# One gathered latent tile in layer 0, and context's retrieval moved ahead of most of the latents' mixer, in a two-layer hybrid trunk

## The chip, the cores and the metric
One NeuronCore of a Trainium2 chip runs the whole program in one launch. The metric is device time in microseconds of one execution, the median of three runs. Less is better. PE is TensorE, DVE is VectorE, ACT is ScalarE, POOL is GpSimd and SP is SyncE, which issues most of the DMAs.

## The reference, cut to what matters
512 latent tokens and 256 context tokens of width 1024 pass two layers. Each layer is a token mixer followed by a PEER feed-forward; both add to the stream through a gate. In layer 0 the mixer is differential attention beside an HGRN2 recurrence. Context reads context alone; latents read both. In layer 1 only the latents go on.

```python
def block(xb):                       # 128 tokens
    q = (xb @ w_q).reshape(P_TOKEN_BLOCK, P_HEADS, 2, P_DQ // 2)
    s = jnp.einsum('nhpd,hpkd->nhpk', q, keys).astype(jnp.float32)
    s_top, i_top = lax.top_k(s, P_TOPK)
...
    gate = jax.nn.softmax(best, axis=-1)
    u = u_tab[idx]
    v = v_tab[idx]
    act = jax.nn.gelu(jnp.einsum('nd,nhkd->nhk', xb, u).astype(jnp.float32), approximate=False)
    return jnp.einsum('nhk,nhkd->nd', (gate * act).astype(v.dtype), v)
```

Eight heads pick 16 experts each, so a token uses 128 of 16,384 experts. An expert is one row of 1024 floats in `u_tab` and one in `v_tab`.

## The kernel before, in words
Everything is float32. A matmul is made of three, over a rounded high part and a rest of each operand (`split`, L221: ScalarE copies the high part, VectorE or POOL subtracts it). `chunk` (L334) loads a 128-column block of a weight matrix (512 KB) on SP's queue and splits it; with `LOS` "p" the rest comes from POOL.

**Two ways through PEER.** *Dense*: for each of 128 blocks j of 128 experts, `expert_in` (L1841) forms gelu(u.x) for all dense tokens (a "u step": 24 matmuls as wide as the dense tokens), the result is multiplied by a gate matrix G, and `peer_out` (L1850) multiplies it with the block's rows of v (an "output step"). G comes from `spread` (L1663), which builds two one-hot matrices for each token on VectorE and ScalarE and multiplies them on PE. 96 of the 128 u steps of layer 0 are done early ("spilled") and stored in AD. *Gathered*: `sparse` (L1693) handles one tile of 128 tokens. For each of its 128 expert slots it gathers one row per token from u (128 x 1024 floats, 512 KB, an indirect DMA that POOL issues, L1711), and one VectorE instruction forms the dot products (L1723). Then the same for v, with an accumulating instruction (L1733). A tile so takes 256 steps, called rows here. `take` (L1716) keeps NS rows in flight.

`GT` says how many latent tiles of a layer are gathered: (0, 2). Context's two tiles are always gathered. With no gathered tile all 512 tokens are dense, and `peer_out` takes its form `full`: 18 matmuls for the first 768 output columns and, by `roll` (L1869), 6 more for the last 256. Otherwise each dense tile of 128 tokens takes 6 matmuls of 512 columns in an output step.

**What sets the order.** Each mixer, tail and retrieval is a generator that yields between pieces. `merge` (L580) takes the next piece from the one that is least far along for its weight. `pull(n)` (L457) emits n further rows of the gathered tiles, first tile first. The engines run in the order that the compiler gives them; each works its own instructions in order.

In `even` (L470) the latents' mixer has four HGRN2 units of 16 steps (64) and four attention units of 7 (28). Beside it runs `tail` (L536): context's output projection (8 steps), its normalisation (1), its retrieval (`retrieve` L1554: 8 heads, then 16 decoding steps), 33 in all. The weights decide who comes first:

```python
left = s.weave([(tail(), TL), (hg, TW * 64), (da, TW * 28)], True)
...
s.rate = RX
s.weave([(hg, left[1]), (da, DF * left[2])])
```

With TW = 3 the mixer ends after 11 steps of the tail; the remaining 22 follow alone. Gathering of context begins only then. `mix_out` (L610) projects the latents and pulls RX = 2 rows in each of its 8 steps.

In `peer(0)` (L1748) the retrieval of four latent tiles pulls 2 x R0 rows at each of its 8 heads. Its other yields carry a price (3.6 for a head of a tile, 2.6 for one of four decoding steps of a tile, 1.2 for one of 32 spreading steps); each time the price passes UP = 5.5 a u step is emitted with R0 rows. The other early u steps follow with RT rows each. `peer_out` spreads what is left evenly.

## Time and profile before

| | us |
|---|---|
| median of 3 runs | 5414.69 |
| runs | 5413.29 to 5420.99 |
| profiled execution | 5428.23 |
| its span, first to last instruction | 5426.4 |
| PE busy | 4376.8 (81%) |
| DVE busy | 4042.6 (74%) |
| POOL busy | 2880.2 (53%) |
| ACT busy | 1924.7 (35%) |

A matmul's duration in the profile holds its passage through the array, which overlaps the next one's. Busy time counts overlapping instructions once. Idle time is put down to what ended it. Times of stretches are from the span's start.

### The profile page before, as it was taken

The page shows a single profiled execution, that of the slowest core. Times are in us where ns is not written, and L with a number is a line of the kernel's source. Part 1 is how long each engine was busy: PE and PEld are TensorE (multiplying, and loading weights), DVE is VectorE, ACT ScalarE, POOL GpSimd, SP SyncE. Part 2 cuts the span into 40 slices and gives each one's busy share as a digit, 9 for nine tenths or more (in the row PEclk, how much of TensorE's full clock was granted, in tenths as well). Part 3 has the DMA queues.
Part 4 walks back from the last instruction along what each step waited for, and adds up shares of the span by engine and source line. Part 5 has one row for each costly group of instructions (what it writes and reads, how often), then busy time and mean ns, then how long its engine had stood idle before and what let it go on. Part 6 is the DMA issues. An engine that isn't in the chain of part 4 may idle for free. (4 is left out here: it accounts for less than half of the span.)

```text
span 5426.4 us, 72537 instructions
## 1 busy us (share of the span) xinstructions
PE 4376.8 (81%) x25323; PEld 3525.1 (65%) x25323; DVE 4042.6 (74%) x8314; ACT 1924.7 (35%) x3942; POOL 2880.2 (53%) x1967
## 2 busy tenths in 40 slices
PE   7889987787877888888898899897947546777766
PEld 5766666566766767777777677785746546555555
DVE  4555669789998546777777676662799987988887
ACT  3444443234553322222222356342415332222222
POOL 2232223564445675655565311442475668899885
PEclk8889998898988999999999999997968777888888
DMA  5431124566657888887788511004376788999996
GB/s 193 138 99 60 58 68 157 195 201 239 222 203 246 294 287 288 281 279 276 268 286 279 186 42 45 16 6 149 100 255 226 277 298 311 345 347 342 347 357 252
DMA packets 450414, 1155.56 MB, mean 213 GB/s; under 512 B 42112, under 2 KB 185856, under 8 KB 446464
## 3 DMA queue, kind: packets, MB, share of 16 engines
q1 hardware_dynamic: 302304, 612.94, 33.9%
q0 software_dynamic: 147744, 537.99, 27.6%
q8 instruction: 200, 3.28, 0.2%
q14 instruction: 166, 1.36, 0.1%
HBM read 1052.20 MB, written 98.57 MB: 212 GB/s over the span
## 5 line engine op out<-in xcount | busy, mean ns | idle before, releaser
L228 POOL TENSOR_TENSOR wlo<-wraw,whi 128x1024 fp32r<-128x1024 f32 x405 | 1003.9, 2482 | 1150.4 <-ACT whi L225 1073.0
L1733 DVE SCALAR_TENSOR_TENSOR sacc<-ga,sact,sacc 128x1024 f32<-128x1024 f32 x508 | 754.8, 1486 | 333.0 <-DMA ga<-in_pv,idx 327.4
L248 PE MATMUL u<-hh,wlo 128*128 128x512 f32 (+1 forms) x2048 | 755.7, 369 | 194.1 <-POOL wlo L228 193.9
L1723 DVE SCALAR_TENSOR_TENSOR ga<-ga,htok 128x1024 f32<-128x1024 f32 x512 | 741.9, 1462 | 203.2 <-DMA ga<-in_pu,idx 202.5
L245 PE MATMUL u<-hh,whi 128*128 128x512 f32 (+1 forms) x2048 | 758.9, 371 | 156.1 <-ACT act L1847 65.3
L1711 POOL DMA_INDIRECT ga<-in_pu,idx x512 | 673.7, 1316 | 356.4 <-DVE ga L1723 103.4
L225 ACT ACTIVATE whi<-wraw 128x1024 fp32r<-128x1024 f32 x415 | 437.1, 1055 | 1093.0 <-PE u L246 490.2
L1711 POOL DMA_INDIRECT ga<-in_pv,idx x512 | 641.9, 1254 | 299.4 <-DVE sacc L1733 121.1
L246 PE MATMUL u<-hl,whi 128*128 128x512 f32 (+1 forms) x2048 | 747.5, 365 | 0.0
L248 PEld LDWEIGHTS u<-hh,wlo 128*128 128x128 f32 x2048 | 435.0, 213 | 256.7 <-POOL wlo L228 214.6
L245 PEld LDWEIGHTS u<-hh,whi 128*128 128x128 f32 x2048 | 435.3, 213 | 226.8 <-ACT act L1847 75.6
L246 PEld LDWEIGHTS u<-hl,whi 128*128 128x128 f32 x2048 | 434.3, 212 | 40.4
L225 ACT ACTIVATE vh<-vraw 128x768 fp32r<-128x768 f32 (+1 forms) x256 | 243.1, 950 | 606.1 <-PE acc L1953 404.2
L1954 PE MATMUL acc<-wh,vl 128*128 128x512 f32 x768 | 314.9, 410 | 69.5 <-DVE vl L228 69.4
L228 DVE TENSOR_TENSOR vl<-vraw,vh 128x768 fp32r<-128x768 f32 (+1 forms) x256 | 334.7, 1307 | 12.4 <-ACT vh L225 12.4
L1688 PE MATMUL g<-ohB,ohA 128*128 128x128 f32 x1536 | 259.1, 308 | 98.4 <-DVE ohB L1686 75.1
L1952 PE MATMUL acc<-wh,vh 128*128 128x512 f32 x768 | 310.3, 405 | 11.0 <-ACT wh L225 11.0
L1688 PEld LDWEIGHTS g<-ohB,ohA 128*128 128x128 f32 x1536 | 227.8, 213 | 135.8 <-issue 57.2
L1953 PE MATMUL acc<-wl,vh 128*128 128x512 f32 x768 | 310.5, 404 | 3.4 <-POOL wl L228 3.4
L1969 PE MATMUL acc<-vl,wh 128*128 128x512 f32 x512 | 223.0, 463 | 109.5 <-DVE vl L228 109.3
L1686 DVE TENSOR_SCALAR ohB<-c_all,pt 128x128 f32<-128x128 f32 x768 | 273.8, 397 | 14.6 <-PE g L1688 12.6
L228 POOL TENSOR_TENSOR wl<-ad,wh 128x512 fp32r<-128x512 f32 (+1 forms) x176 | 235.7, 1340 | 58.0 <-ACT wh L225 56.0
(506 smaller groups left out, 9774.0 us busy)
## 6 DMA issues: line engine op xcount, KB each, us to landing
wraw<-in_uT SPq DMA_DIRECT2D x256, 512.0 KB
vraw<-in_pv SPq DMA_DIRECT2D x256, 512.0 KB
wraw<-in_ada_w SPq DMA_DIRECT2D x96, 512.0 KB
G<-stg SPq DMA_DIRECT2D x24, 2048.0 KB
wraw<-in_ew SPq DMA_DIRECT2D x64, 512.0 KB
G<-G SPq DMA_DIRECT2D x32, 1024.0 KB
wraw<-in_pwq SPq DMA_DIRECT2D x48, 512.0 KB
AD<-act SPq DMA_DIRECT2D x96, 256.0 KB
```

The lines of the kernel that those rows point to most:

```text
L225: nc.scalar.activation(hi, x, AF.Copy)
L228: i = (lo_eng or nc.vector).tensor_tensor(lo, x, hi.bitcast(F32), OP.subtract)
L245: nc.tensor.matmul(o, a, hh[:, k], start=(k == 0), stop=False)
L246: nc.tensor.matmul(o, a, hl[:, k], start=False, stop=False)
L248: nc.tensor.matmul(o, b, hh[:, k], start=False, stop=(k == nk - 1))
L1688: nc.tensor.matmul(ps[:, n], A, B, start=True, stop=True)
L1711: nc.gpsimd.indirect_dma_start(out=ga, out_offset=None, in_=tab, in_offset=bass.IndirectOffsetOnAxis(ap=idx[:, k:k + 1], axis=0))
L1723: nc.vector.scalar_tensor_tensor(ga, ga, 1.0, htok, op0=OP.mult, op1=OP.mult, accum_out=act[:, k:k + 1])
L1733: nc.vector.scalar_tensor_tensor(acc, ga, act[:, k:k + 1], acc, op0=OP.mult, op1=OP.add)
L1952: nc.tensor.matmul(acc[d], a, wh, start=st, stop=False)
L1953: nc.tensor.matmul(acc[d], a, wl, start=False, stop=False)
L1954: nc.tensor.matmul(acc[d], b, wh, start=False, stop=sp)
```

## The change
Layer 0 gathers one latent tile of four, so 384 tokens are dense and `full` no longer holds. TW falls from 3 to 0.4: the whole tail is woven with the first two fifths of the latents' mixer. `weave` returns the steps taken; the rest of the mixer runs with RX = 3.5 rows pulled after every step, and the projection with RM = 4 rows a step. Rows in flight: NS from (3, 5) to (4, 7); layer 0's PEER adds NP = 3 buffers and its output steps NX = 3 (before 1); `take` now looks as far ahead as there are buffers. In `spread` the small tile pt moves from the pool of six buffers to one of two. R0 and RT of layer 0 rise from 2 to 2.5.

```diff
--- before.py
+++ after.py
@@ -25,16 +25,17 @@
 SPILL = (96, 80)
 JG = 4
 UP = (5.5, 4.0)
-GT = (0, 2)
-R0 = (2.0, 2.5)
+GT = (1, 2)
+R0 = (2.5, 2.5)
 RG = (2, 1)
 NR = 2
 NV = 3
 VQ = 'sync'
 OH = "av"
 VERB = 0
-TW = 3
-RX = 2.0
+TW = 0.4
+RX = 3.5
+RM = 4.0
 NE = 6
 ND_ = 3
 PW = 2
@@ -42,12 +43,12 @@
 DL = 8
 LA = 3
 NA = 3
-NX = 1
+NX = 3
 ROB = 1e-5
 MORE = tuple(tuple(int(c) for c in x) for x in '11,11'.split(','))
 MOREP = tuple(tuple(int(c) for c in x) for x in '00,00'.split(','))
 TP = 3.6
-RT = (2, 2.5)
+RT = (2.5, 2.5)
 LOS = 'ppv,p,p,p,p,p,p'.split(',')
 NG = (1, 1)
 SQ = 'sync'
@@ -61,7 +62,8 @@
 MO = tuple(int(c) for c in '00')
 UB = 2
 AH = 2
-NS = (3, 5)
+NS = (4, 7)
+NP = (3, 0)
 TB = 32
 
 
@@ -546,7 +548,7 @@
                         yield from s.mix_out(mps, s.stream(YC, L), L, yh, yl, I['ewo'], put)
                         yield from s.ctx_peer(cx, mps, psp)
                     with s.more(*M2):
-                        left = s.weave([(tail(), TL), (hg, TW * 64), (da, TW * 28)], True)
+                        took = s.weave([(tail(), TL), (hg, TW * 64), (da, TW * 28)], True)
                 sp1 = s.side.enter_context(tc.tile_pool(name="sp1", bufs=NS[0], side="right"))
                 s.sp2 = s.side.enter_context(tc.tile_pool(name="sp2", bufs=1, side="right"))
                 s.gpools = [sp1] * NS[0]
@@ -557,8 +559,9 @@
                 s.gens = [s.sparse(0, s.sp2, s.pick[i], s.HT[i], keep(i)) for i in range(2)]
                 for g in s.gens:
                     next(g)
-                s.rate = RX
-                s.weave([(hg, left[1]), (da, DF * left[2])])
+                for _ in s.merge([(hg, max(1, 64 - took[1])), (da, max(1, 28 - took[2]))]):
+                    s.pull(RX)
+                s.rate = RM
             if s.until == 'diff':
                 nc.sync.dma_start(out=s.O['y'], in_=YX)
                 return
@@ -600,7 +603,7 @@
         done = [0] * len(gens)
         for _ in s.merge(gens, until, done):
             pass
-        return [max(1, n - b) for (_, n), b in zip(gens, done)]
+        return done
 
     def add_to(s, x, g):
         def put(d, ps):
@@ -1660,13 +1663,13 @@
             yield from decode(i)
             yield from after(i)
 
-    def spread(s, p, sp, psp, gps, pick, tb0, G):
+    def spread(s, p, p2, sp, psp, gps, pick, tb0, G):
 
         nc, C = s.nc, s.C
         tp = s.t(psp, [128, 3, 128], tag='hs')
         for i in range(3):
             s.flip(tp[:, i], pick[i].rearrange("p a b -> p (a b)"))
-        pt = s.t(p, [128, 3, 128], tag='pt')
+        pt = s.t(p2, [128, 3, 128], tag='pt')
         nc.scalar.activation(pt, tp, AF.Copy)
         for b in range(128 // TB):
             stg = s.t(sp, [128, 128, TB], tag='stg')
@@ -1715,7 +1718,7 @@
 
         def take(tab, k):
 
-            while len(ahead) < NS[l] and k + len(ahead) < 128:
+            while len(ahead) < len(s.gpools) and k + len(ahead) < 128:
                 ahead.append(fetch(tab, k + len(ahead)))
             return ahead.pop(0)
         for k in range(128):
@@ -1770,6 +1773,8 @@
                 sp1 = ent(tc.tile_pool(name=s.name("sp1"), bufs=NS[l]))
                 s.sp2 = ent(tc.tile_pool(name=s.name("sp2"), bufs=1))
                 s.gpools, s.turn = [sp1] * NS[l], 0
+            if NP[l]:
+                s.gpools = s.gpools + [ent(tc.tile_pool(name=s.name("spx"), bufs=NP[l]))] * NP[l]
             HT = tc.dram_tile([max(ng, 1), 128, D], F32, name=s.name('HT'))
 
             old = [j for j in range(128) if (j + 1) * spill // 128 > j * spill // 128]
@@ -1810,6 +1815,7 @@
                 def done():
                     et.close()
                     eg.append(ee(tc.tile_pool(name=s.name("pe2"), bufs=NE, side="right")))
+                    eg.append(ee(tc.tile_pool(name=s.name("pe3"), bufs=2, side="right")))
                     eg.append(ee(tc.tile_pool(name=s.name("pe1"), bufs=NG[l], side="right")))
 
                 def after(i):
@@ -1820,7 +1826,7 @@
                                                lambda acc: s.add_tok(psu, 'u', acc, s.xl, t0, gl)))
                         next(s.gens[-1])
                         return
-                    yield from s.spread(eg[0], eg[1], psm, gps, s.pick[i], t0 // TB, G)
+                    yield from s.spread(*eg, psm, gps, s.pick[i], t0 // TB, G)
                 price, n = 0.0, 0
                 for p in s.retrieve(l, ep, tp_, pk, (psq, 'q'), (psm, 'hs'), (hh, hl), tiles, 1 if ctx else ng, done, after):
                     price += p
@@ -1861,7 +1867,7 @@
                 tc.tile_pool(name=s.name("ad"), bufs=ND_) as ad, \
                 tc.tile_pool(name=s.name("ppo"), bufs=1, space=PSUM) as pso:
             acc = [s.t(pso, [128, 512], tag=f'acc{i}') for i in range(6 if full else ND // 64)]
-            s.gpools = s.gpools + [sp3] * NX
+            gpools, s.gpools = s.gpools, s.gpools + [sp3] * NX
             s.rate = s.left() / (128.0 + 128 - len(old)) + 0.02
             dm = 768 if full else D
             prev = []
@@ -1971,7 +1977,7 @@
                             nc.tensor.matmul(acc[2 * t + e], b, vh[:, e * 512:e * 512 + 512], start=False, stop=sp)
                 s.pull(s.rate)
             s.pull(1 << 20)
-            s.gpools = s.gpools[:NS[l]]
+            s.gpools = gpools
             if full:
                 roll(1, pend)
                 for d in range(6):
```

## Rows read from the trace of the kernel before

**Rows 1.** Eight stretches: length, busy us (instructions) by engine, clock, DMA share, GB/s
```profile
340.00:862.00 522.00, 474.42 (x2626) 349.27 (x2624) 322.83 (x820) 227.55 (x459) 146.30 (x77) 0.96 0.22 67
862.00:965.00 103.00, 76.49 (x455) 62.81 (x456) 99.55 (x379) 24.94 (x47) 32.74 (x15) 0.80 0.49 170
965.00:1800.00 835.00, 657.49 (x3176) 529.92 (x3176) 730.75 (x2077) 355.46 (x878) 433.68 (x264) 0.88 0.66 223
1800.00:2035.00 235.00, 208.21 (x886) 164.80 (x885) 106.40 (x100) 63.33 (x94) 175.37 (x103) 0.97 0.88 297
2035.00:3060.00 1025.00, 918.31 (x3803) 740.17 (x3804) 746.68 (x907) 262.29 (x440) 579.64 (x428) 0.95 0.81 278
...
3830.00:4490.00 660.00, 417.57 (x2565) 380.77 (x2563) 614.70 (x1657) 240.19 (x554) 406.85 (x246) 0.80 0.70 238
4490.00:4580.00 90.00, 59.58 (x332) 54.79 (x332) 62.08 (x38) 17.47 (x25) 79.92 (x48) 0.79 0.89 304
4580.00:5390.00 810.00, 596.68 (x2630) 474.62 (x2631) 718.37 (x704) 238.74 (x349) 696.84 (x485) 0.85 0.95 344
```

**Rows 2.** POOL groups, 340 to 862: count | busy us, mean ns | idle before <-releaser
```profile
L228 POOL TENSOR_TENSOR wlo<-wraw,whi 128x1024 fp32r<-128x1024 f32 x50 | 121.9, 2439 | 301.6 <-ACT whi L225 268.8 <-issue 18.7 <-PE hs L799 9.4
```

**Rows 3.** Groups of instructions, 965 to 1800
```profile
L1723 DVE SCALAR_TENSOR_TENSOR ga<-ga,htok 128x1024 f32<-128x1024 f32 x128 | 198.4, 1553 | 54.9 <-DMA ga<-in_pu,idx 54.6
...
L1686 DVE TENSOR_SCALAR ohB<-c_all,pt 128x128 f32<-128x128 f32 x499 | 168.2, 378 | 10.8 <-PE g L1688 9.4 <-ACT pt L1670 0.2
...
L1685 DVE TENSOR_SCALAR ohA<-c_all,pt 128x128 f32<-128x128 f32 x249 | 75.1, 308 | 1.0 <-PE g L1688 0.4
...
L1733 DVE SCALAR_TENSOR_TENSOR sacc<-ga,sact,sacc 128x1024 f32<-128x1024 f32 x43 | 69.1, 1606 | 27.2 <-DMA ga<-in_pv,idx 27.0
...
L1847 ACT ACTIVATE act<-u 128x512 f32<-128x512 f32 x61 | 35.6, 584 | 0.0
```

**Rows 4.** Groups of instructions, 1800 to 2035
```profile
L1733 DVE SCALAR_TENSOR_TENSOR sacc<-ga,sact,sacc 128x1024 f32<-128x1024 f32 x71 | 93.9, 1323 | 128.4 <-DMA ga<-in_pv,idx 127.1
...
L228 POOL TENSOR_TENSOR wlo<-wraw,whi 128x1024 fp32r<-128x1024 f32 x35 | 85.0, 2429 | 11.8 <-ACT whi L225 11.2
...
L1847 ACT ACTIVATE act<-u 128x512 f32<-128x512 f32 x36 | 20.9, 580 | 4.1 <-issue 4.1
```

**Rows 5.** Groups of instructions, 2035 to 3060, VectorE
```profile
L1733 DVE SCALAR_TENSOR_TENSOR sacc<-ga,sact,sacc 128x1024 f32<-128x1024 f32 x140 | 193.6, 1383 | 116.2 <-DMA ga<-in_pv,idx 114.6
...
L1723 DVE SCALAR_TENSOR_TENSOR ga<-ga,htok 128x1024 f32<-128x1024 f32 x128 | 163.3, 1295 | 104.4 <-DMA ga<-in_pu,idx 104.4
...
L228 DVE TENSOR_TENSOR vl<-vraw,vh 128x768 fp32r<-128x768 f32 x126 | 139.1, 1104 | 0.5 <-ACT vh L225 0.5
...
L1878 DVE SCALAR_TENSOR_TENSOR xl<-u,g,xl 128x512 f32<-128x512 f32 x126 | 93.6, 743 | 3.8 <-PE u L1876 3.8
...
L228 DVE TENSOR_TENSOR rl<-vraw,rh 128x256 fp32r<-128x256 f32 x124 | 91.7, 778 | 0.0
```

**Rows 6.** Timeline near 1838: start, us, engine, line, operation
```profile
1838.01 2.52 POOL L228 TENSOR_TENSOR wlo<-wraw,whi 128x1024 fp32r<-128x1024 f32 x1 [1.37 <-ACT whi L225]
...
1838.18 2.63 DVE L228 TENSOR_TENSOR rl<-vraw,rh 128x256 fp32r<-128x256 f32 x1
```

**Rows 7.** Timeline of PE, two matmuls, the second 22 after the first
```profile
2408.93 0.39 PE L245 MATMUL u<-hh,whi 128*128 128x512 f32 x1
...
2413.92 0.39 PE L1953 MATMUL acc<-wl,vh 128*128 128x512 f32 x1
```

**Rows 8.** Instructions on tile rl: duration ns min/median/max, first and last start
```profile
L228 DVE TENSOR_TENSOR rl<-vraw,rh x128: 407/414/2629, 1834.5 to 3050.8; 128x256 fp32r<-128x256 f32 x128
```

**Rows 9.** DMA issues by line, with count and KB of each
```profile
G<-G SPq DMA_DIRECT2D x32, 1024.0 KB
...
ad<-AD SPq DMA_DIRECT2D x96, 256.0 KB
```

**Rows 10.** Windows, one slice of layer 1
```profile
4352.00:4488.00 136.00, 69.87 (x442) 66.55 (x443) 118.38 (x187) 45.72 (x118) 84.27 (x62) 0.71 0.84 297
```

## The prediction

> **What bounds the kernel now.** I read the busy times by stretch first [rows 1]. They follow the program: latents' mixer with context's projection beside it (340 to 862), context's retrieval and the latents' output projection (862 to 965), layer 0's PEER in three parts (965 to 1800 retrieval and one-hot spreading, 1800 to 2035 the rest of the 96 spilled u steps, 2035 to 3060 the 128 output steps), and for comparison three stretches of layer 1, which already gathers two of its four tiles. The reader is to see that each part has another bound. 340 to 862 is PE's (474 of 522 us) while VectorE is at 62% and DMA at 0.22. 862 to 1800 is VectorE's (99.6 of 103, 731 of 835). 2035 to 3060 is PE's (918 of 1025). 4580 to 5390, where PE has less to do, is DMA's: share 0.95 at 344 GB/s.
>
> Next come the groups of instructions [rows 3 to 5]. Every gathered row costs VectorE one pass over 1024 elements, POOL one issue and DMA 512 KB. 128 + 43 rows run before 1800, 71 before 2035, and the remaining 270 after (268 in the two groups, two first ones apart). VectorE waits for landing rows: 55 + 27 us, 127 us of 235, and 104 + 115 us [rows 3 to 5]. The queue is three rows deep there.
>
> **The change, part by part.** Sums are made against the profiled execution, 5428.2 us, which lies 13.5 us above the median of 5414.7.
>
> *Mixer and context (340 to 965, now 625 us).* Latent mixer steps number 64 + 28 = 92; the context tail has 33. With weights 0.4 x 64 and 0.4 x 28 the tail ends beside 26 + 11 = 37 steps, leaving 55, each followed by 3.5 rows: 193 rows.
> First part: PE 474.4 x 37/92 = 191, and at most the 76.5 of 862 to 965 [rows 1], 267 together, at the 0.91 busy share of 340 to 862: 290 us. VectorE has 130 + 99.6 = 230 in it and fits beside. The tail's loads, splits and stores are moved ahead of most of the mixer's on SP and POOL: DMA at 0.22 and POOL at 28% hide them; if that cover were gone, the 24 splits would cost 24 x 2.44 = 59 us [rows 2].
> Second part: PE has only 474.4 x 55/92 = 284. VectorE has 322.8 x 55/92 = 193 and 193 rows x (1.295 + 0.08) = 266; 0.08 is my allowance for reading the accumulator. That is 459, and 495 us at the 0.93 busy share of 3830 to 4490 [rows 1], where rows fill the gaps of other VectorE work. Below it is bounded by full hiding, 470 at a share of 0.977. Above, no hiding: 55 x 522/92 + 266 = 578. I take 495, nearest to the stretch that mixes the two kinds of work.
> Here a row matters: a VectorE split of 256 elements, 0.41 us at the median [rows 8], took 2.63 us when it started 0.17 us behind a POOL split, and ended 0.1 us after it [rows 6]. Two-input work on the two engines takes turns. The duration of 1.295 has such waits in it, from a stretch with POOL at 57%.
> The Trainium skill, GPSIMD Engine Reference, section 1 (Specifications), says that GpSimd shares its SBUF interfaces with VectorE and contends with VectorE instructions of two SBUF inputs, as the rows' are. The trace agrees [rows 6]. Counted in full, that rule would add the 19 weight splits of this part, 19 x 2.44 = 46 us, so 505 instead of 459, 542 instead of 495, and no gain in the sum.
> Output projection: 103 us now, PE 76 busy, its adds waiting behind the retrieval on VectorE. Without the retrieval but with 32 rows (44 us of VectorE): 85.
> 290 + 495 + 85 = 870 against 625: **+245**.
>
> *Retrieval and u steps (965 to 2035, now 1070 us).* One tile fewer is spread: a quarter of 168.2 + 75.1 [rows 3], 61 us of VectorE. By the prices of the yields, 3 x 8 x 3.6 + 4 x 4 x 2.6 + 3 x 32 x 1.2 = 243, 44 u steps fit in at 5.5 each. Rows: 8 x 5 at the projections and 44 x 2.5, so 150 instead of 171: 21 x 1.57 = 33. Together 94, or 107 at the 0.875 share. Lookahead grows from 3 to 7; half of the 82 us of waiting should go, 40. 835 - 147 = 688, call it 690. 52 u steps with 130 rows follow, against 36 steps now [rows 4]. A step now takes 235/36 = 6.5 us. It will hold 2.5 rows. POOL: 175.4/36 = 4.9 now, which with half a row of 1.2 more is 5.5. DMA: 3.5 x 512 + 192 KB = 2.03 MB, at 344 GB/s 5.9. PE: 24 matmuls of 384 columns, 4.1. I take 6.0, 312 us; 5.5 and 6.5 are the ends (286 to 338). 690 + 312 = 1002: **-68**. The new transposes, copies and eight 64 KB stores of the gathered tile fall in the normalisation and are counted below.
>
> *Output steps (2035 to 3060, now 1025 us).* Matmuls of 512 columns follow one another every 4.99/22 = 0.227 us [rows 7]. Now 24 a step and 24 more in 32 of them. Afterwards 18 a step and 24 of 384 columns (0.17 us, scaled): 128 x 18 x 0.227 + 32 x 24 x 0.17 = 654 us against 871. VectorE loses the rolled adds and small splits (93.6 + 91.7) and a third comes onto its large ones (139.1 x 1/3 = 46) [rows 5]: 747 becomes about 600. Rows left: 768 - (193 + 32) - (150 + 130) = 263, so VectorE keeps that load. DMA [rows 9]: 128 x (512 + 192) + 96 x 192 + 32 x 512 + 263 x 512 KB = 266 MB, which at 344 GB/s is 773 us, now the largest. Ten rows ahead should keep it fed. I take 800; 773 is the lower end. **-225**.
>
> *Rest.* Closing copies, transposes and adds of three dense tiles, and the gathered tile's preparation: about **+10**, an estimate. Layer 1: lookahead 5 becomes 7, then 10. VectorE waited little there and DMA is at 0.95 in 4580 to 5390: **-10**, between -45 and +10. Moving pt to a two-buffer pool and larger NX, NP only take memory; pt is written once a tile, so nothing waits.
>
> Sum: 245 - 68 - 225 + 10 - 10 = -48. 5428.2 - 48 = 5380; less 13.5, about **5367 us** in the median's terms.
>
> **The rivals.** *Rows stand in line with the mixer (slower).* A POOL gather waits until VectorE has finished the row whose buffer it takes; behind it on POOL stands the weight split of the next projection, and PE waits for that. Then rows and steps add up: 578 instead of 495, +83, 5450 us. It decides from 543 us in that part on, 9.9 us a step. For it: mixer steps have round trips between VectorE, ScalarE and PE in them that no row can fill. Against: 3830 to 4490 reaches 0.93 with such a mixture.
> *The output steps lose TensorE's clock (slower).* The mean granted clock was 0.95 in 2035 to 3060 with PE 90% busy, 0.85 in 4580 to 5390 with PE 74% busy, and 0.71 in the slice from 4352 with PE half busy [rows 1, 10]: means over the levels 1.2 and 2.4 GHz, fallen where PE stood still more. At 0.85 the 654 us become 769, still under 800; at 0.71 they become 921, and the time 5367 + 121 = 5488.
> The Trainium skill, TensorE: Matmul & The Clock Gate, part 1, says that an idle array falls to half its clock and recovers only with sustained work. The trace agrees in direction [rows 1, 10], and that rule speaks against this change.
> *All covers hold (faster).* 470 in the mixer, 275 ahead of it, 286 for the u steps, 773 for the output, -45 in layer 1: 25 + 15 + 26 + 27 + 35 = 128 less, 5240 us.
> *Rows do not start early.* If they start only with the output projection, 193 rows of 512 KB go to the output steps: 101 MB, 294 us at 344 GB/s, so 1094 where I have 800, while the mixer's second part costs 312 instead of 495. 5367 + 294 - 183 = 5478.
>
> **How the numbers follow.** Chances: my forecast 0.52, rows in line 0.22, clock 0.08, all covers 0.15, no early start 0.03. A measurement here tells 0.2% (11 us) from no change. My forecast's own terms are uncertain by about 50 us: of its 0.52, 0.42 is faster, 0.06 same and 0.04 slower. With 0.15 from the covers, faster is 0.57. Of the 0.33 of the other three, 0.31 is slower and 0.02 same: 0.35 and 0.08. The range runs from 5245, just above the case in which all covers hold, to 5475, beyond rows in line. It leaves out the clock's case, the late start and some of the best.
>
> **What would show it.** Right: no row before the context's retrieval ends at about 630; 3.5 rows per mixer step and VectorE over 90% busy until about 1125; the PEER normalisation near 1210 instead of 965; about 1000 us to the first output step; DMA over 0.9 and PE below 85% in the output steps, about 800 us long; layer 1's PEER unchanged within 45 us. Wrong: VectorE under 85% in the mixer's second part, or output steps over 870 us with DMA under 0.85. Output steps under 750 us would need more than 350 GB/s.

## The result, and the profile after

The change made the kernel slower: 5575.74 us (5567.14 to 5586.55, 4 runs) against 5417.84 beside it, ratio 1.0283 [1.0254, 1.0311]. The profiled execution spans 5580.2 us against 5426.4, 153.8 more. Its stretches, with the columns of [rows 1]:

```profile
340.00:680.00 340.00, 288.33 (x1520) 221.83 (x1521) 235.96 (x806) 122.47 (x253) 114.24 (x59) 0.87 0.26 85
680.00:1177.00 497.00, 316.32 (x1296) 213.15 (x1294) 412.98 (x708) 133.08 (x247) 282.37 (x218) 0.71 0.69 231
1177.00:1300.00 123.00, 72.62 (x448) 52.03 (x448) 72.02 (x55) 26.42 (x33) 73.21 (x49) 0.79 0.77 270
1300.00:1935.00 635.00, 492.73 (x2596) 444.42 (x2597) 610.17 (x1708) 284.24 (x709) 368.80 (x225) 0.87 0.68 237
1935.00:2260.00 325.00, 211.27 (x1009) 196.28 (x1007) 249.08 (x293) 66.69 (x94) 280.95 (x176) 0.85 0.91 320
2260.00:3201.00 941.00, 750.80 (x3084) 617.19 (x3085) 642.13 (x654) 232.99 (x322) 541.87 (x419) 0.89 0.78 284
4714.00:5550.00 836.00, 606.60 (x2708) 484.28 (x2707) 710.10 (x716) 239.25 (x353) 691.06 (x486) 0.86 0.91 336
```

The reader is to see two things. The mixer with context takes 340 + 497 us and the output projection behind it 123, together 960 up to the PEER normalisation of the latents; the kernel before takes 671 (522 for the mixer, 149 for retrieval and projection up to that normalisation at 1011; the 103 of [rows 1] end 46 us ahead of it). And in 2260 to 3201, the output steps, nothing is full: PE 80% of the time, VectorE 68%, POOL 58%, DMA 0.78. The forecast for them was 800 us at a DMA share over 0.9.

From landmarks in the timelines (VectorE's first step of the latents' PEER normalisation, its first weighting, the product with G, in the output steps, the last output matmul, layer 1's PEER normalisation, the end), the difference of 154 splits so:

| stretch | before | after | difference | predicted |
|---|---|---|---|---|
| up to the normalisation | 1011 | 1300 | +289 | +245 |
| retrieval and u steps | 1023 | 960 | -63 | -68 |
| output steps | 1027 | 941 | -86 | -225 |
| to layer 1's PEER | 721 | 729 | +8 | +10 |
| layer 1's PEER to the end | 1644 | 1650 | +6 | -10 |

So the output steps are where the expected gain is missing. Their groups in the changed kernel, against [rows 5]:

```profile
L1975 PE MATMUL acc<-vl,wh 128*128 128x512 f32 x768 | 337.9, 440 | 163.3 <-DVE vl L230 163.3
...
L1736 DVE SCALAR_TENSOR_TENSOR sacc<-ga,sact,sacc 128x1024 f32<-128x1024 f32 x134 | 205.1, 1530 | 71.1 <-DMA ga<-in_pv,idx 69.5
L1726 DVE SCALAR_TENSOR_TENSOR ga<-ga,htok 128x1024 f32<-128x1024 f32 x128 | 180.7, 1434 | 72.0 <-DMA ga<-in_pu,idx 71.7
L230 DVE TENSOR_TENSOR vl<-vraw,vh 128x1024 fp32r<-128x1024 f32 x126 | 168.8, 1339 | 79.8 <-ACT vh L227 79.8
...
L227 ACT ACTIVATE vh<-vraw 128x1024 fp32r<-128x1024 f32 x126 | 132.4, 1051 | 407.1 <-PE acc L1977 397.2 <-issue 9.9
...
L230 POOL TENSOR_TENSOR wlo<-wraw,whi 128x1024 fp32r<-128x1024 f32 x32 | 85.3, 2665 | 223.2 <-ACT whi L227 223.1
L1894 DVE TENSOR_TENSOR ad<-ad,G 128x384 f32<-128x384 f32 x96 | 68.8, 720 | 65.1 <-DMA ad<-AD 65.1
...
L230 POOL TENSOR_TENSOR wl<-act,wh 128x384 fp32r<-128x384 f32 x32 | 33.4, 1042 | 91.5 <-ACT wh L227 91.5
```

VectorE still waits 70 + 72 us for rows (219 in all before), with ten buffers instead of four. PE waits 163 us for vl, the low half of the output weights, which VectorE makes between rows. ScalarE's vh, the high half, waits for PE, and POOL waits 223 + 91 us for ScalarE ahead of two kinds of split. The engines stand in a ring. The timelines of POOL, of VectorE, and of PE and ScalarE show one turn of it (start, us, engine, line, operation, idle before):

```profile
2517.12 1.30 POOL L1714 DMA_INDIRECT ga<-in_pu,idx  x1 [0.30 <-issue]
2528.60 3.12 POOL L230 TENSOR_TENSOR wlo<-wraw,whi 128x1024 fp32r<-128x1024 f32 x1 [10.17 <-ACT whi L227]
2533.98 1.01 POOL L230 TENSOR_TENSOR wl<-act,wh 128x384 fp32r<-128x384 f32 x1 [2.25 <-ACT wh L227]
2535.14 0.95 POOL L1714 DMA_INDIRECT ga<-in_pu,idx  x1
```

```profile
2528.25 1.22 DVE L1726 SCALAR_TENSOR_TENSOR ga<-ga,htok 128x1024 f32<-128x1024 f32 x1
...
2529.39 3.41 DVE L1726 SCALAR_TENSOR_TENSOR ga<-ga,htok 128x1024 f32<-128x1024 f32 x1
...
2541.64 1.23 DVE L1726 SCALAR_TENSOR_TENSOR ga<-ga,htok 128x1024 f32<-128x1024 f32 x1 [4.70 <-DMA ga<-in_pu,idx]
```

```profile
2517.67 0.80 PE L1975 MATMUL acc<-vl,wh 128*128 128x512 f32 x1 [5.25 <-DVE vl L230]
...
2523.44 1.06 ACT L227 ACTIVATE vh<-vraw 128x1024 fp32r<-128x1024 f32 x1 [10.16 <-PE acc L1977]
2527.45 1.06 ACT L227 ACTIVATE whi<-wraw 128x1024 fp32r<-128x1024 f32 x1 [2.95 <-PE u L248]
```

PE had stood 5.25 us for vl, and ScalarE stands 10.16 us for PE ahead of vh, with whi behind it. POOL stands 10.17 us ahead of wlo, because whi is late, with the next fetch behind wlo in its queue. In these 17 us (2518.42 to 2535.14) no fetch is issued; VectorE uses up what has landed, and then waits 4.70 us for a row. Over all 262 rows of this part that could be paired with their fetch, the fetch was issued 7.6 us (median) before use, with 4 in flight, against 7.4 us and 3 before.

### The profile page after: what moved, and what is told of

Its sections match the earlier page's. It is cut to its first block, busy times and chain, and to the rows that moved or that the text cites. A ratio compares the mean times of both kernels' runs of the same rounds, so it can differ in the third digit from the quotient of the medians.

```text
span 5580.2 us, 70344 instructions
## 1 busy us (share of the span) xinstructions
PE 4178.5 (75%) x24336; PEld 3426.0 (61%) x24336; DVE 4232.9 (76%) x8278; ACT 1861.1 (33%) x3684; POOL 3165.3 (57%) x2223
## 3 DMA queue, kind: packets, MB, share of 16 engines
q14 instruction: 164, 1.34, 0.1%
## 5 line engine op out<-in xcount | busy, mean ns | idle before, releaser
L250 PE MATMUL u<-hh,wlo 128*128 128x384 f32 (+1 forms) x2048 | 705.8, 345 | 273.4 <-POOL wlo L230 272.8
L247 PE MATMUL u<-hh,whi 128*128 128x384 f32 (+1 forms) x2048 | 705.2, 344 | 169.7 <-ACT act L1853 89.7
L1975 PE MATMUL acc<-vl,wh 128*128 128x512 f32 x1280 | 570.7, 449 | 273.9 <-DVE vl L230 267.9
L248 PE MATMUL u<-hl,whi 128*128 128x384 f32 (+1 forms) x2048 | 693.0, 338 | 0.0
L1974 PE MATMUL acc<-vh,wh 128*128 128x512 f32 x1280 | 553.6, 435 | 46.0 <-ACT vh L227 26.0
L1975 PEld LDWEIGHTS acc<-vl,wh 128*128 128x128 f32 x1280 | 275.2, 216 | 377.6 <-DVE vl L230 313.0
L227 ACT ACTIVATE vh<-vraw 128x1024 fp32r<-128x1024 f32 x256 | 269.1, 1052 | 560.0 <-PE acc L1977 535.3
L230 DVE TENSOR_TENSOR vl<-vraw,vh 128x1024 fp32r<-128x1024 f32 x256 | 364.1, 1423 | 108.2 <-ACT vh L227 108.2
L1977 PE MATMUL acc<-vh,wl 128*128 128x512 f32 x1280 | 422.8, 428 | 16.7 <-POOL wl L230 16.7
L1974 PEld LDWEIGHTS acc<-vh,wh 128*128 128x128 f32 x1280 | 275.3, 215 | 113.7 <-ACT vh L227 35.7
```

The costliest lines, as they stand in the source:

```text
L227: nc.scalar.activation(hi, x, AF.Copy)
L230: i = (lo_eng or nc.vector).tensor_tensor(lo, x, hi.bitcast(F32), OP.subtract)
L247: nc.tensor.matmul(o, a, hh[:, k], start=(k == 0), stop=False)
L248: nc.tensor.matmul(o, a, hl[:, k], start=False, stop=False)
L250: nc.tensor.matmul(o, b, hh[:, k], start=False, stop=(k == nk - 1))
L1974: nc.tensor.matmul(o, a, vh[:, c], start=st, stop=False)
```

## The experiments

Landmarks of each run's profile, output steps by difference, and times (medians; ratio to the kernel before beside it; runs without a ratio were timed once). The mark of the first output step lies up to 4 us ahead of its first weighting; in e16 it lies 12 us ahead, as VectorE stood for G, and its output steps count 1095 from the weighting itself.

| run | normalis. | first output step | last output matmul | output steps | us | ratio |
|---|---|---|---|---|---|---|
| before | 1011 | 2034 | 3061 | 1027 | | |
| after | 1300 | 2260 | 3201 | 941 | 5575.7 | 1.0283 [1.0254, 1.0311] |
| e1 tile only | 1027 | 1973 | 3102 | 1128 | 5480.7 | 1.0094 [1.0062, 1.0127] |
| e2 order only | 1299 | 2313 | 3184 | 870 | 5560.9 | 1.0242 [1.0221, 1.0263] |
| e8 tail ahead | 1063 | 2016 | 3146 | 1131 | 5526.0 | 1.0184 [1.0167, 1.0201] |
| e4 no rows | 1299 | 2255 | 2945 | 690 | 5325.9 | 0.9818 [0.9798, 0.9838] |
| e3 third vh | 1301 | 2256 | 3153 | 897 | 5516.9 | 1.0160 [1.0142, 1.0178] |
| e6 short vector | 1298 | 2257 | 3130 | 873 | 5510.6 | |
| e7 quarter fetched | 1298 | 2258 | 3133 | 875 | 5504.8 | |
| e9 both cuts | 1298 | 2254 | 3134 | 881 | 5507.5 | |
| e12 wlo on VectorE | 1303 | 2261 | 3162 | 901 | 5529.2 | 1.0175 [1.0150, 1.0200] |
| e13 POOL rows only | 1297 | 2251 | 3144 | 893 | 5516.2 | 1.0149 [1.0123, 1.0174] |
| e14 and vh, ad | 1299 | 2256 | 3099 | 843 | 5467.1 | 1.0071 [1.0043, 1.0099] |
| e17 and raw, ad | 1301 | 2260 | 3110 | 850 | 5488.3 | 1.0102 [1.0078, 1.0126] |
| e5 deep before | 1038 | 2001 | 3018 | 1017 | 5391.4 | 0.9943 [0.9928, 0.9959] |
| e10 the same, rotated | 1040 | 2001 | 3023 | 1022 | 5388.7 | 0.9923 [0.9904, 0.9942] |
| e11 with third vh | 1039 | 1999 | 3079 | 1080 | 5441.4 | 1.0012 [1.0000, 1.0024] |
| e15 layer 0's queue | 1033 | 1996 | 3029 | 1033 | 5398.2 | 0.9931 [0.9908, 0.9954] |
| e16 and POOL rows only | 1039 | 1993 | 3100 | 1108 | 5478.3 | 1.0079 [1.0058, 1.0101] |
| e18 and raw, ad | 1038 | 1997 | 3022 | 1024 | 5386.0 | 0.9903 [0.9886, 0.9921] |

**The parts of the change.** Tile only (the tail beside all of the mixer, no rows with it):

```diff
-TW = 0.4
+TW = 3
-RM = 4.0
+RM = 2.0
```


> The new kernel with the weaving of before (TW 3, RM 2): one latent tile is gathered, but no row runs beside the mixer. My theory: the move of the rows beside the mixer costs (+289 us there) what the smaller dense part cannot pay back. Then the mixer's stretch returns to the time of before, PEER's normalisation begins near 1011 us as before, and the output steps get about 470 rows instead of 263; at the 344 GB/s of layer 1 that is at least 1090 us, I expect 1100 to 1250 instead of 941. Total 5430 to 5580 us. Rival (the dense part itself is what fails, whatever the rows): output steps stay near 941 and the total falls to about 5300.

Order only (no tile of the latents gathered):

```diff
-GT = (1, 2)
+GT = (0, 2)
-NX = 3
+NX = 1
-NP = (3, 0)
+NP = (2, 0)
```


> The new kernel with no latent tile gathered (GT 0): 512 tokens stay dense, the order and the rows beside the mixer are the new ones (fewer row buffers, NP 2 and NX 1, for lack of memory). The mixer's stretch should last as in the new kernel, about 290 us longer than before. Hardly any row is left for the output steps, so these show what 512 dense tokens cost without rows: my theory says 870 to 930 us (PE's 871 us of columns), 100 to 150 less than before. Total 5560 to 5680. Rival (moving the rows pays by itself): total under 5420.

Windows of the output steps, of the first and of the second:

```profile
1973.00:3102.00 1129.00, 806.42 (x3087) 636.62 (x3086) 933.15 (x944) 234.54 (x324) 886.40 (x631) 0.87 0.92 334
```

```profile
2313.00:3184.00 871.00, 864.13 (x3806) 715.45 (x3807) 490.22 (x515) 260.53 (x441) 249.81 (x162) 1.00 0.53 168
```

Neither half gains, and both times lie in the ranges of their theories. The tile alone puts 472 rows into the output steps, and there DMA is full (0.92 of 1129 us); it costs 54 us by the medians. The order alone (with the longer queue, and R0 and RT at 2.5) empties the output steps of rows, which gives 871 us with PE busy for 864, but loses 288 us ahead of the normalisation; it costs 134. With 384 dense tokens 941 - 690 (e4, below) = 251 us are due to 255 rows (262 against 7), 0.98 each; with 512 dense tokens 1027 - 870 = 157 us to 265 rows (269 against 4), 0.59 each.

Tail ahead of the mixer, and no row beside it:

```diff
-RX = 3.5
-RM = 4.0
+RX = 0.0
+RM = 2.0
```


> The new kernel without rows beside the mixer (RX 0, RM 2), context's tail still ahead of most of it. Against the run with one tile gathered and the old weaving it shows the move of the tail alone. Theory: the retrieval gains nothing by the move, since it was hidden behind the latents' output projection in part; the mixer ends near 1000 us instead of 863 and PEER's normalisation begins near 1120 instead of 1027; the rest is as in that run, so total about 5570. The rows beside the mixer then cost the difference to 1177, 0.9 us each. Rival (the move of the tail is free and rows alone lengthen the mixer): normalisation begins by 1030, total about 5480.

Moving the tail alone costs 1063 - 1027 = 36 us against e1, between the theory (normalisation at 1120) and the rival (1030); that the tail's waits are no longer covered by the whole mixer is likely, but not shown. The rest of the loss ahead of the normalisation comes with the rows: 1300 - 1063 = 237 us for 208 rows (227 against 19 by then), 1.14 us each. In the output steps, which had 471 rows instead of 262, the difference is 1131 - 941 = 190, 0.91 each. So the move loses: a row is not cheaper beside the mixer than where it came from.

How much of a row the mixer hides can be read between the same two marks, the end of context's retrieval (678 in both) and the first split of the latents' output projection, in e8 and then in the changed kernel:

```profile
678.00:975.00 297.00, 252.34 (x1310) 174.04 (x1309) 167.88 (x389) 117.97 (x236) 45.75 (x24) 0.89 0.16 55
```

```profile
678.00:1186.00 508.00, 318.27 (x1304) 214.25 (x1302) 414.16 (x711) 134.52 (x249) 284.07 (x219) 0.71 0.70 233
```

VectorE's rows in that part of the changed kernel:

```profile
L1726 DVE SCALAR_TENSOR_TENSOR ga<-ga,htok 128x1024 f32<-128x1024 f32 x128 | 164.4, 1299 | 46.1 <-DMA ga<-in_pu,idx 45.6
...
L1736 DVE SCALAR_TENSOR_TENSOR sacc<-ga,sact,sacc 128x1024 f32<-128x1024 f32 x66 | 87.5, 1325 | 12.7 <-DMA ga<-in_pv,idx 12.3
...
L1726 DVE DVE_READ_ACCUMULATOR ga<-ga,htok 128x1 f32 x128 | 10.3, 81 | 0.0
```

The 195 rows (a first one stands apart) take 262 us of VectorE, and the part is 211 us longer: four fifths of the rows' time were paid, 1.08 us each. PE's matmuls are the same; its clock fell from 0.89 to 0.71 and its busy time rose by 66 us. Twelve loads of ScalarE's function table (last section) are in these 211 us.

**What a row costs in the output steps.** The tile's rows left out; a third split buffer; VectorE's passes cut to an eighth; three fetches of four left out; both cuts:

```diff
# e4, in peer_out
+            if l == 0:
+                s.gens.pop()
+                s.todo -= 256
# e3
-tc.tile_pool(name=s.name("pv"), bufs=2) as pvp
+tc.tile_pool(name=s.name("pv"), bufs=3 if l == 0 else 2) as pvp
-NX = 3
+NX = 1
# e6, with s.cut true in layer 0's output steps; likewise for acc
+            w = 128 if s.cut else D
+            nc.vector.scalar_tensor_tensor(ga[:, 0:w], ga[:, 0:w], 1.0, htok[:, 0:w], ...
# e7; e9 has this and e6
-                ahead.append(fetch(tab, k + len(ahead)))
+                j = k + len(ahead)
+                ahead.append(ahead[-1] if s.cut and j % 4 and ahead else fetch(tab, j))
```


> The new kernel without the gathered latent tile's rows: that tile's share of the PEER sum is left out, and with it 256 row steps in layer 0's output steps. If the rows are what holds the output steps (late rows or VectorE's time), they fall from 941 to about 735 us, PE's 654 us of columns at a clock of 0.89. If the hand-over of two buffers holds them by itself, they stay over 820. Total 5370 or 5460.

> The new kernel with three buffers instead of two for the split rows of v in layer 0's output steps (and one row buffer fewer there). Theory: PE's 163 us of waiting for VectorE's split come from the hand-over of two buffers (PE must be done with step n before step n+2 is split, on VectorE behind rows). Then the output steps shrink from 941 to 780 to 860 us and the total to 5410 to 5510. Rival (late rows block VectorE, whatever the buffers): less than 25 us change.

> The new kernel; in layer 0's output steps each row is fetched whole, but VectorE works on its first 128 of 1024 elements only, so seven eighths of that arithmetic are left out there. If a row's price of 0.98 us (941 us with 262 rows, 690 without) is VectorE's time, the output steps fall to 720 to 790 us. If it is the landing of rows, they stay at 880 to 941.

> The new kernel; in layer 0's output steps only every fourth row is fetched and used four times, so VectorE's work is whole while three quarters of the transfers and of POOL's issues are left out (the sum is over the wrong rows). If the price is VectorE's time, the output steps stay at 860 to 941 us. If it is transfers, they fall to 720 to 790.

> The changed kernel with both cuts at once, in layer 0's output steps alone: VectorE works on 128 of a row's 1024 elements, and three rows of four are not fetched (the last fetched one is used again). Separately each took 66 to 68 us from the 941 us of these steps; leaving the rows out altogether took 251. Theory (a row's price is VectorE's pass, the late landing and POOL's issue behind one another in the order of the queues, so the parts add): the two together take 130 to 180 us, output steps of 760 to 810, span 5400 to 5450. Rival (both cuts remove the same wait, in which VectorE stands at a row ahead of the weight split): together little more than one of them, 70 to 100 us, output steps of 840 to 870, span 5480 to 5510. What would be left over the 690 us without rows is then the price of a row's bare instructions, its issue on POOL and its short passes with their accumulator reads.

Without rows the steps take 690 us, less than the 735 expected, at a granted clock of 0.99. Each cut alone takes 66 to 68 us: e6 ends just under its range for late rows, e7 in its range for VectorE's time, and neither comes near 720 to 790. With both cuts the steps take 881, no less than with one. e3 (897) lies between its theory and its rival; it gave up two row buffers, not one as its expectation says. Windows of e4 and of e9:

```profile
2255.00:2945.00 690.00, 672.30 (x3072) 568.79 (x3073) 292.25 (x261) 234.19 (x321) 234.52 (x163) 0.99 0.60 193
```

```profile
2254.00:3134.00 880.00, 725.77 (x3078) 604.08 (x3079) 396.03 (x654) 233.18 (x321) 290.75 (x225) 0.91 0.56 188
```

In e9 VectorE is busy 396 us of 880, DMA 0.56, POOL 291. A quarter of the transfers and an eighth of the elements still cost 190 us. The theory fails; the rival comes nearest (840 to 870), and what is left is waiting, not work of VectorE, POOL or DMA. Two of its groups show waits:

```profile
L230 POOL TENSOR_TENSOR wlo<-wraw,whi 128x1024 fp32r<-128x1024 f32 x32 | 76.6, 2396 | 487.1 <-ACT whi L227 487.1
...
L1729 DVE SCALAR_TENSOR_TENSOR ga<-ga,htok 128x128 f32<-128x128 f32 x128 | 38.0, 300 | 60.7 <-DMA ga<-in_pu,idx 57.8
```

VectorE still waits 58 us for 32 fetched rows of this group (and 62 for as many of the other), and POOL stands 487 us ahead of wlo. The cuts had not touched that order. The length of POOL's wait by itself proves little, though: in e4, without rows, POOL stands 364 us there and ScalarE's vh 208 us for PE, and the steps take 690.

**POOL's queue.** First the 32 low halves of the u weights, then also the 128 of the steps' own weights, moved from POOL to VectorE:

```diff
# e12
-LOS = 'ppv,p,p,p,p,p,p'
+LOS = 'ppv,p,p,p,p,v,p'
# e13, besides
-                s.split(a, wh, wl, lo_eng=nc.gpsimd)
+                s.split(a, wh, wl, lo_eng=nc.vector if l == 0 else nc.gpsimd)
```


> The changed kernel with the 32 low halves of the u weights in layer 0's output steps split on VectorE and not on POOL. In the changed kernel POOL stands 223 us in these steps ahead of those splits and 91 us ahead of the low halves of the weights that come from u steps, each time because ScalarE is late, and the row fetches behind them on POOL leave late: 4 rows in flight at use with 10 buffers, 7.6 us from issue to use. That wait doesn't depend on how long a row's pass or transfer is, so it also explains why both cuts together took no more than one. Theory (the rows' lateness comes from POOL's order): part of the blocks is gone, VectorE's waits for rows fall from 141 us to 70 to 110, and though VectorE gets 32 x 1.25 = 40 us more, the output steps come to 880 to 925, span 5520 to 5560. Rival (VectorE now stands at those splits itself, in the same order behind ScalarE): 960 to 1010, span 5600 to 5650.

> As the last run, and the 128 low halves of the output steps' weights (384 tokens) also on VectorE: in layer 0's output steps POOL then does nothing but fetch rows. VectorE gets 32 x 1.25 + 128 x 0.56 = 112 us more, and loses about 50 by no longer taking turns with POOL (262 rows and 126 splits, 0.1 to 0.3 us each): some 700 of it. Theory (the rows' lateness comes from POOL's order): rows are issued 15 us or more ahead of use, VectorE's waits for them fall under 60 us from 141, the output steps come to 830 to 890, span 5470 to 5530. Rival (VectorE's own order is what couples rows and matmuls, so more work on it only adds): 980 to 1040, span 5620 to 5680.

e12's time falls within its theory (901), but not for the theory's reason: POOL then stood 338 us ahead of wl made from u steps, so that rows were no earlier (7.9 us) and VectorE waited 138 us for them, not 70 to 110. What gave the 40 us is not separated; the 32 splits took 1.35 us each on VectorE for 2.67 on POOL, and VectorE's row passes fell to 1.40 and 1.36 us. In e13 rows are issued 26.8 us ahead with 9 in flight, and VectorE's busy time falls to 621 us though it has 107 us of splits more, as a row's pass takes 1.22 to 1.28 us instead of 1.43 to 1.53. Output steps and groups:

```profile
2251.00:3144.00 893.00, 723.05 (x3064) 603.70 (x3064) 620.52 (x813) 239.24 (x322) 364.73 (x259) 0.89 0.86 300
```

```profile
L1975 PE MATMUL acc<-vl,wh 128*128 128x512 f32 x768 | 328.5, 428 | 153.5 <-DVE vl L230 153.5
...
L1736 DVE SCALAR_TENSOR_TENSOR sacc<-ga,sact,sacc 128x1024 f32<-128x1024 f32 x134 | 171.6, 1280 | 5.0 <-DMA ga<-in_pv,idx 3.5
...
L1726 DVE SCALAR_TENSOR_TENSOR ga<-ga,htok 128x1024 f32<-128x1024 f32 x128 | 152.8, 1217 | 0.0
...
L1894 DVE TENSOR_TENSOR ad<-ad,G 128x384 f32<-128x384 f32 x96 | 52.7, 553 | 209.8 <-DMA ad<-AD 163.8 <-issue 45.8
```

The wait for rows is gone (141 to 4 us) and another stands in its place: 164 us for u results read back (ad). PE waits for vl almost as long as before, so the steps came down by 48 only, 3 us beyond the expectation. Of these, 40 had come in e12 with rows as late as ever; the step to e13, with rows in time and 69 us of further splits on VectorE, gave 8 more. SP's queue may have a part in the wait for ad. Its waits in the changed kernel (line, what it waited for: us, times, longest):

```profile
SPq L1924 <- DVE vl L230: 468.7, 103, 13.9
SPq L1922 <- POOL wl L230: 176.4, 64, 8.2
```

SP stands at loads of raw output weights (L1924), whose buffer VectorE frees with vl, and reads of ad, the stored u results, stand behind them. Two ways to loosen that, on top of e13:

```diff
# e14
-ND_ = 3
+ND_ = 5
-... name=s.name("pv"), bufs=2) as pvp
+... name=s.name("pv"), bufs=3 if l == 0 else 2) as pvp
-NX = 3
+NX = 1
-NP = (3, 0)
+NP = (2, 0)
# e17
-ND_ = 3
+ND_ = 5
-NV = 3
+NV = 5
-NX = 3
+NX = 1
```


> As the run in which POOL does nothing but fetch rows in layer 0's output steps, with a third buffer for the split output weights and five buffers, not three, for the u results read back; for these the rows' queue gives up three buffers (9 in place of 10 would be too many: 7 remain, and rows were landed 20 us before use). In that run VectorE waited 4 us for rows but 164 us for the u results read back, and the matrix unit 154 us for the low halves. Theory (the steps go in lock-step, so each wait taken away shows the next; with three taken away the largest resource decides, DMA, 773 us by the prediction's bytes): output steps 780 to 850, span 5400 to 5480. Rival (at a DMA share of 0.86 the transfers already set the pace of the last run): 860 to 895, span 5480 to 5520.

> As the run in which POOL does nothing but fetch rows in layer 0's output steps (893 us, VectorE waiting 164 us for u results read back), with five buffers, not three, for the raw output weights and for the u results read back, and two split buffers as in the change; the rows' queue gives up two of ten. In that run SP's queue stood 307 us at the load of raw output weights, whose buffer VectorE frees with the split vl, and the reads of u results stand behind it. Theory (VectorE waits for a transfer that SP could not issue because it waited for VectorE): with raw weights five steps ahead VectorE's wait for u results falls under 60 us and the output steps to 800 to 850, span 5425 to 5480. Rival (the transfers are late because DMA is busy, share 0.86): 870 to 895, span 5495 to 5520.

Output steps and two groups of e14, then the output steps of e17:

```profile
2256.00:3099.00 843.00, 721.64 (x3063) 595.85 (x3062) 618.12 (x813) 227.46 (x321) 375.07 (x259) 0.93 0.89 316
```

```profile
L227 ACT ACTIVATE vh<-vraw 128x1024 fp32r<-128x1024 f32 x125 | 131.5, 1053 | 324.8 <-DMA vraw<-in_pv 187.4 <-PE acc L1977 93.4 <-PE u L248 21.2
...
L1894 DVE TENSOR_TENSOR ad<-ad,G 128x384 f32<-128x384 f32 x96 | 53.1, 554 | 162.3 <-DMA ad<-AD 158.2 <-DMA G<-G 4.0
```

```profile
2260.00:3110.00 850.00, 712.41 (x3062) 594.66 (x3061) 621.42 (x813) 238.01 (x322) 387.87 (x258) 0.91 0.89 313
```

Both reach the range of their theories, 843 and 850 us (e17's span, 5485 us, lies 5 above it). But the wait for ad did not go: 158 us in e14, and 161 in e17, where under 60 was expected and SP stood 314 us at the loads of raw weights, no less than in e13 (307). In e14 ScalarE now waits 187 us for raw weights to land and 93 for PE (377 in e13). With DMA at 0.89 and 316 GB/s the transfers come near to those of layer 1 in the changed kernel (0.91, 336 GB/s). How much of the last 40 to 70 us over 773 to 800 is the order of SP's queue and how much DMA's load stays open.

**The longer queue in the kernel before.** Order and tiles of before with after's queue; the same with new buffers put first when the list grows; and a third vh buffer:

```diff
# e5, against the changed kernel
+TW = 3; RM = 2.0; GT = (0, 2); R0 = (2.0, 2.5); RT = (2, 2.5); NX = 1; NP = (2, 0)
# e10, besides
+    def grow(s, pool, n):
+        o, t = s.gpools, s.turn % max(1, len(s.gpools))
+        s.gpools, s.turn = [pool] * n + o[t + 1:] + o[:t + 1], -1
# e11, besides
-NP = (2, 0)
+NP = (1, 0)
+... name=s.name("pv"), bufs=3 if l == 0 else 2) as pvp
```


> Order, dense tokens and rates of before (GT 0, TW 3, R0 and RT 2, RM 2); of the change only the deeper queue of rows remains (NS 4 and 7, look-ahead over all buffers, NP 2, NX 1: 6 ahead in layer 0's PEER, 7 in its output steps, instead of 3). Theory: a row costs VectorE's time and its place in line more than its lateness; rows cost the 512-token output steps 156 us for 272 rows, of which the waits for late rows on VectorE are only covered time. Then the output steps fall from 1027 by 10 to 50 us, the u steps before them by 10 to 30, the total to 5360 to 5410. Rival (the rows' lateness is the price): output steps near 900, total under 5300.

> The kernel before in order and tiles (no tile of the latents gathered, tail beside all of the mixer, no rows with the mixer) with the longer queue of rows alone: 4 rows ahead in retrieval, 6 in the u steps, 7 in the output steps, against 3, 3 and 4. Where the list of buffers grows, the new buffers now come first, so that no buffer is taken whose row is still awaited. Theory (rows waited for were late because the queue was short; output steps then keep their 1020 us or so): 5380 to 5405, faster than before by 0.3 to 0.7%. Rival (the gain of the earlier run came from the order in which buffers were taken): 5410 to 5425.

> As the run with the longer queue alone (the order and tiles of before), with a third buffer for the split output weights in layer 0 and one row of the queue given up for it in the u and output steps (5 and 6 rows). In the changed kernel the third buffer took 44 us from the output steps, where two rows of the queue were given up for it. Theory (matrix unit waits for the low half of the weights in the order of VectorE's queue): output steps 20 to 50 us shorter than with the longer queue alone, 5345 to 5380. Rival (with 512 dense tokens PE is 90% busy in these steps and has nothing to give): 5385 to 5410, no better than the longer queue alone.

With the longer queue (in both layers here) the kernel is faster than before, and the order of its buffers is not why (5391 and 5389). The gain lies in the retrieval and u steps, 961 us against 1023, less 29 us by which the normalisation is later; the output steps hardly move. The third vh buffer, 44 us better in e3, is 58 us worse here, which misses theory and rival. PE no longer waits for vl (78 us in e10), but 109 us, not 22, for the buffer that VectorE frees with the adds of the rolled columns:

```profile
L247 PE MATMUL u<-hh,whi 128*128 128x512 f32 x248 | 120.0, 484 | 109.4 <-DVE xl L1889 109.4
```

The row buffer given up may have a part in it: VectorE waits 261 us for rows, 202 in e10.

Then the kernel before itself, with layer 0's queue alone (4, 5, 6 buffers), with POOL cleared as in e13, and with more raw buffers:

```diff
# e15, against the kernel before; grow as above
-NS = (3, 5)
+NS = (4, 5)
+NP = (1, 0)
-            while len(ahead) < NS[l] and k + len(ahead) < 128:
+            while len(ahead) < (len(s.gpools) if l == 0 else NS[l]) and k + len(ahead) < 128:
# e16, besides: LOS and lo_eng as e13, ND_ = 5
# e18, as e15, besides: NV = 4, ND_ = 4
```


> The kernel before, with nothing changed but layer 0's queue of rows: 4 buffers in retrieval, 5 in the u steps, 6 in the output steps, against 3, 3 and 4. Theory (rows are late in part because the queue is short): output steps about 1020, 5395 to 5415, faster by 0.3 to 0.7%. Rival (the gain of the longer queue needs 7 buffers, or came from the other edits of that run): 5425 to 5440, the same as before.

> As the last run (order and tiles of before, longer queue), and in layer 0's output steps all low halves of weights are split on VectorE, so that POOL only fetches rows there, with five buffers for the u results read back. VectorE gets 29 x 1.22 + 128 x 0.7 = 125 us on its 760 of 1022, and loses some 50 by no longer taking turns with POOL. Theory (the rows' lateness comes from POOL's order, with 512 dense tokens too): output steps 960 to 1000, 5335 to 5385. Rival (VectorE at 835 beside 917 of the matrix unit, each in the other's order, has no room left): 1020 to 1060, 5400 to 5450.

> The kernel before with layer 0's longer queue of rows (4, 5 and 6 buffers; 5398 us) and four buffers, not three, for raw output weights and for u results read back, in both layers. SP's queue stood some 550 us in layer 0's output steps at loads of raw weights. Theory (the same loop of SP and VectorE holds here): output steps 985 to 1020 in place of 1033, and something in layer 1: 5340 to 5385. Rival (with 512 dense tokens VectorE waits 213 us for rows and only 40 for u results, so these loads are early enough): 5390 to 5410.

e15 (5398) lies in its theory's range, so layer 0's longer queue is enough for the gain. e16 misses, and is slower than even its rival had it (1020 to 1060, 5400 to 5450). Its groups:

```profile
L1724 DVE SCALAR_TENSOR_TENSOR ga<-ga,htok 128x1024 f32<-128x1024 f32 x128 | 151.2, 1217 | 2.0 <-DMA ga<-in_pu,idx 2.0
...
L246 PE MATMUL u<-hh,whi 128*128 128x512 f32 x248 | 119.5, 482 | 155.7 <-DVE xl L1885 155.7
...
L1895 DVE TENSOR_TENSOR ad<-ad,G 128x512 f32<-128x512 f32 x96 | 66.1, 691 | 247.3 <-DMA ad<-AD 229.4 <-DMA G<-G 10.9 <-issue 4.6
```

Rows are in time (2 us), but VectorE waits 229 us for ad and PE 156 us for VectorE's adds. With 512 dense tokens PE is busy for 923 us, so that it has less time in which to wait; that this is the reason is argued, not shown. In e18 the output steps stay at 1024 (985 to 1020 expected), and its time lies between theory and rival; by the medians, in different comparisons, it is 12 us faster than e15, with intervals that overlap. e5, e10, e15 and e18 are faster than both kernels; e18 has the lowest median, 1.0% [0.8, 1.1] below the kernel before, but its interval overlaps those of e10 and e15.

## Why the prediction was right or wrong

The time, 5575.7 us, lies outside the range and on the other side. Step by step:

- *Mixer and context, +245.* Measured +289. The second part took 497 us for 495, but that was luck: VectorE was busy 413 us, not 459 (the rows took 262 of it, as forecast, the mixer 151 for 193), and 83% of the time, not 93%. Under 85% was a sign of being wrong that I had named. The mixer's rest alone is 297 us (e8) and not 312, and four fifths of the rows' time came on top. The first part took 340 for 290: PE was busy 288 us (267 forecast), at a share of 0.85 for 0.91 and a clock of 0.87 for 0.96. The projection, by the same marks before and after, took 26 less (123 for 149), where 18 less was forecast. The order of events was as described: first row at 685 us, normalisation at 1300 where I had 1210 from a base that I read 46 us early.
- *Retrieval and u steps, -68.* Measured -63; first output step 960 us behind the normalisation, for "about 1000".
- *Output steps, -225: the step that failed.* "Ten rows ahead should keep it fed. I take 800": they took 941 (with DMA under 0.85, the sign that I had named for this), and that is 139 of the 202 us by which the sum missed. The bytes were right: 284 GB/s x 941 us is 267 MB for 266. Wrong was that the largest resource, DMA, would set the time, with the rest beside it: an eighth of VectorE's pass and a quarter of the transfers (e9) still left 881 us. The queue had ten buffers but 4 rows in flight, because fetches stand on POOL behind splits that wait for ScalarE, which waits for PE, which waits for vl, which stands on VectorE behind the row. Freed of that (e13) the rows were in time, but the steps still took 893; with more buffers for vh and ad (e14) they took 843. So 98 of the 139 us came back with the same rows and nearly the same work on VectorE (618 us for 642). How the 98 divide among the single waits and VectorE's shorter passes, and what holds the rest, stays open. Without rows the steps took 690, with PE busy 672 for 654, so the dense part was judged well.
- *Layer 1, -10.* Measured +6; its DMA share even fell, 0.95 to 0.91.
- *Rows stand in line with the mixer* (0.22, 5450) was to decide from 543 us in that part; it took 497. By the mark it did not occur, by the mechanism it did in the main: 211 of the rows' 262 us came on top of the mixer, where the forecast had 183 of 266. It was not by the path described: POOL waited 68 + 49 us there for VectorE's rows, but PE only 15 us for POOL's splits.
- *Clock loss* (0.08, 5488). It came about in part: 0.89 granted, 751 us busy where 672 are needed at 0.99 (e4). By these rows a stall of PE is paid more than once: 79 us of longer matmuls on top of 172 us more of idle PE (190 against 18). The Trainium skill, TensorE: Matmul & The Clock Gate, part 1, says that an idle array falls to half its clock. The trace agrees in direction: 0.99 granted with PE busy 97% of the time (e4), 0.89 with 80%.
- *Covers hold* and *rows do not start early* did not occur.
- Two readings were off without consequence: the split of [rows 6] ended 0.28 us behind POOL's, not 0.1, and 267 us at a share of 0.91 make 294, not 290.

The prices that the experiments gave explain the sign of the total. 256 rows more at about 1 us each cost what one dense tile less gives back: e1 against before is +0.9%. And moving rows beside the mixer changes only at what price they run.

Even with the output steps at 843 (e14) the change stays 0.7% [0.4, 1.0] behind: the loss ahead of the normalisation (288 us) is larger than the gain behind it.

## What to carry to other kernels

A queue's depth in buffers is no depth in flight: look at how long before its use a transfer is issued, and at what stands ahead of that issue on the issuing engine's queue. Where in-order engines wait for each other in a ring, times of the resources don't overlap down to the largest; take the price of the added work from a stretch that already mixes it with that partner, or cut it out on the chip (e4), before moving it. A wait removed from such a ring uncovers the next (rows, then read-back, then raw weights), so a repair gives less than its wait measures (e13: 48 us for 137, and 40 of the 48 came before the wait had gone). A forecast time can come out right with its mechanism wrong: check the terms (413 us of VectorE for 459), not only their sum (497 for 495).

## What had not been expected

The Gelu of a row tile, which now falls into the mixer, costs ScalarE its function table. The kernel before loads a table 19 times, the changed one 35 times, 16 x 1.283 = 20.5 us more; 14 loads fall between 1009 and 1295 us: the Gelu's own, eleven in the mixer's chains of Exp and Ln, and two in the normalisation behind it. Groups of 680 to 1177:

```profile
L649 ACT ACT_TABLE_LOAD x2 | 2.6, 1283 | 0.0
...
L269 ACT ACT_TABLE_LOAD x2 | 2.6, 1283 | 0.0
...
L1728 ACT ACT_TABLE_LOAD x1 | 1.3, 1283 | 0.0
```

Ahead of that Gelu (1009 us) the same functions ran without a load; behind it a Ln and the Exp that follows it took one each (1063.5 and 1065.5 us). e2, with the same order, has the same 35, and e1 and e8, with the rows behind the mixer, 19. What these loads cost the span was not tried. The Trainium skill, ScalarE activation tables: per-element evaluation and per-set limits, section "What a function is on this engine", says that functions of different sets are one load of 1283 ns apart and that those of one set need none. The trace agrees in the size of a load; which set a load brings it does not show.

The turn-taking of [rows 6] is worth more than I had allowed: with POOL free of splits (e13) VectorE's row passes fell from 1.43 and 1.53 us to 1.22 and 1.28, 262 rows x 0.23 = 60 us, and vl from 1.34 to 1.22. The pass of 3.41 us in the timeline above ran beside POOL's wlo of 3.12. The Trainium skill, GPSIMD Engine Reference, section 1 (Specifications), says that GpSimd contends with VectorE instructions of two SBUF inputs, as these passes are; these runs agree, with that price.
